# A streaming-encoder layer with a mixture of experts: short convolution in PSUM, VectorE alone converting weights late in the mixers, the first experts' chunks converted earlier, GpSimd out of the routing

## The chip, the core and the metric

The kernel runs on one core of a Trainium2 chip. The metric is the device time of one execution in microseconds (us). The engines in the text are TensorE (PE; its weight loads are PEld), VectorE (DVE), ScalarE (ACT), GpSimd (POOL) and SyncE (SP), whose queue issues every weight transfer.

## What is computed

One layer over 256 frames of width 1024. Three mixers read the same input projection, are gated and summed, and go through one output projection; a layer norm follows, and then 16 experts, two of which each frame uses.

```python
a  = a_val * sigmoid(a_gate)                       # branch A, "A" chunks
a  = silu(layer_norm(conv31(a) + conv_a_b))        # 31 taps per channel
yb = gate_bb * conv3(gate_cc * xb)                 # branch B, "X" and "B" chunks
pooled = trailing means over 2/4/8/16 minus self   # branch C, "C" chunks
merged = g0 * (a @ w_a_out) + g1 * (yb @ w_b_out) + g2 * (pooled @ w_c) * c_scale
x = layer_norm(ALPHA * x + merged @ w_o + b_o)
probs = softmax(x @ w_router + b_router)           # best group, best 2 in it
y = sum over e of combine[:, e] * (silu(x @ w_gate[e]) * (x @ w_up[e])) @ w_down[e]
x = layer_norm(ALPHA * x + y)
```

## The kernel before, in words

All weights are cut into chunks of 128 x 2048 float32 (1 MB), in the order of use: 49 for the mixers (`MIX`), 96 for the experts (`EXP`, six for each). Mixer chunks 0 to 7 are "A", 8 to 11 "C", 12 to 23 four times X, X, B, 24 is "WC", 25 to 36 four times G1, G2, WB, 37 to 40 "G0", and 41 to 48 WA, WA, WO, WA, WA, WO, WO, WO.

A chunk is not multiplied as it comes. It is split into a rounded half (H, `hi`, a copy on ACT, line 162) and the rest (L, `lo`, a subtraction, line 172), and TensorE multiplies three pairs: H with both halves of the activations, L with one. One mixer chunk is 48 matmuls of 256 columns (lines 314 and 319). `convert` runs two chunks ahead of the products; with `CUT = 1280` GpSimd subtracts 1024 + 256 of the 2048 columns and VectorE 768. Exceptions are the "native" chunks: the second half of every expert's down projection but the last is multiplied unsplit, as float32, by `mm_native` (line 1022).

In the mixers VectorE also evaluates the 31-tap convolution, one instruction for one tap of 128 channels (lines 333 and 336, accumulating in PSUM in tiles "z"). The taps wait in a list, and `drain` hands out as many for each chunk as a budget of 5.0 us less the chunk's own cost (`COST`) allows. The short convolution of branch B is done in `ev_X`: a product into u (line 396), then three taps from u into a tile y in SBUF (lines 400 and 402); `ev_B` multiplies the gate in (line 407). At chunk `LNA` (32) the taps that remain are handed out, and the layer norm of branch A follows at set distances from there (`ln_a`: line 458 to 487); its result AH, AL is the operand of the WA chunks. Up to line 800 a scheduler reorders instructions within each engine's queue; from `manual_schedule` on, the order is as written.

Then comes the routing. Two tiles of 128 frames (t = 0, 1) get their output projection (`wo`), residual (`add1`), statistics, logits, softmax, choice of experts, and places; `gather2` collects the chosen frames, and the first expert starts. `warm_up` puts idle matmuls in between. `C0`, `C1`, `C2` are the first three converted expert chunks. In the expert loop ACT rounds and VectorE alone subtracts, each two instructions of 1024 columns for a chunk.

Weight slots: `give` puts a free slot's name into a list, and SP issues the next chunk's transfer into it, so a transfer starts when a slot comes free. Slots H0 to H2 and L0 to L2 hold the split halves until the routing; after that all slots are one pool.

Of the kernel before, what the change touches and what calls it, by code (L numbers as in the profile page):

```python
# [49 lines left out]
def native(j):  # L50

    return CHUNKS[j][0] == "ED" and CHUNKS[j][2] == 1 and CHUNKS[j][1] < NE - 1
# [60 lines left out]
def body(ctx, tc, w, xt, x, par, rows, out):  # L113
# [211 lines left out]
    CA = {}  # L325

    def conv_tap(i, k):

        src = UP[:, i, k:k + T]
        wk = P[:, PCW + i * TAPS + k:PCW + i * TAPS + k + 1]  # L330
        if k == 0:
            CA[i] = bank("z", (128, T))
            V.tensor_scalar(CA[i], src, wk, col(PCB, i), op0=OP.mult, op1=OP.add)
        else:
            ca = CA[i]
# [50 lines left out]
    yconv = {}  # L386
    Y = {}

    def ev_X(i, p):
        if i == 0:  # L390
            Y["h"], Y["l"] = slot("YH", [128, KT, T], F32R), slot("YL", [128, KT, T], F32R)
        cc = t2k([128, T])
        S.activation(cc, p[:, 0], AF.Identity, bias=col(PB, 24 + i))
        u = t2k([128, 2 + T])
        G.memset(u[:, :2], 0.0)
        V.scalar_tensor_tensor(u[:, 2:], p[:, 1], col(PB, 32 + i), cc, op0=OP.add, op1=OP.mult)  # L396
        if i % 2 == 0:
# [129 lines left out]
    LNA = 32  # L527
# [6 lines left out]
    COST = {"A": .45, "C": .7, "X": 1.3, "B": .9, "WB": .7, "WA": 1.3}  # L534
# [24 lines left out]
    def router_consts():  # L559
# [8 lines left out]
        pb = bank("pj", (128, 2, NE))  # L568
# [229 lines left out]
    acc = {}  # L798
    ctx.enter_context(tc.manual_schedule())
# [39 lines left out]
    dummy = small([128, 1])  # L839
    for h in range(2):  # L840
# [3 lines left out]
        stats1(0, 2 * h, 2 * h + 1)  # L844
    S.activation(dummy, X1[:, 0, :1], AF.Exp)
# [7 lines left out]
    convert(C0, 2048, 512)  # L853
    hold[0] = 3
# [6 lines left out]
    x1a(0, 1)  # L861
    logits(0, 0)
# [3 lines left out]
    softmax1(0, u0)  # L866
    x1b(0, 0)
# [3 lines left out]
    select(0)  # L871
    wo(NM - 2, 2, 1, 1)
# [35 lines left out]
    lo(C1, G, 0, 1024)  # L908
# [76 lines left out]
    def hidden(e):  # L985
# [13 lines left out]
        def parts():  # L999
            S.activation(HS[e][:, :, 0], HF[e], AF.Copy)  # L1000
# [104 lines left out]
    for e in range(NE + 1):  # L1105
# [44 lines left out]
        if e:  # L1150
            p0 = bank("pj", (128, 512))
            block(lambda j: mm(p0, lambda k: HS[e - 1][:, k], j, True, True), before=gu if e < NE else ())
            steps = [lambda: ev_down(e - 1, 0, p0)]
# [9 lines left out]
            p1 = block(lambda j: down1(e - 1, j, some), before=steps, between=parts)  # L1163
# [5 lines left out]
            last = [lambda e=e, p1=p1: ev_down1(e - 1, p1)]  # L1169
# [6 lines left out]
    p1 = block(lambda j: down1(NE - 1, j, None))  # L1176
    ev_down1(NE - 1, p1)
# [113 lines left out]
```

## Time and profile before

| | us |
|---|---|
| median of 3 runs (lowest, highest) | 633.08 (632.39, 633.84) |
| the profiled execution's own time | 633.34 |
| its span, first to last instruction | 631.6 |
| PE, PEld busy in it | 585.9, 485.5 |
| DVE, ACT, POOL busy in it | 569.9, 373.8, 254.1 |

Busy shares of the whole span say little here, since the stages have different limits. The table by stretches of time is to be read first: in each stretch the number of matmuls in brackets, against a stretch in which TensorE never waits, tells how much of it was lost; the granted clock tells how much of that was lost to a slower clock, and the waits tell whom TensorE waited for.

### The profile page before, as it was taken

The page shows a single profiled execution, that of the slowest core. Times are in us where ns is not written, and L with a number is a line of the kernel's source. Part 1 is how long each engine was busy: PE and PEld are TensorE (multiplying, and loading weights), DVE is VectorE, ACT ScalarE, POOL GpSimd, SP SyncE. Part 2 cuts the span into 40 slices and gives each one's busy share as a digit, 9 for nine tenths or more (in the row PEclk, how much of TensorE's full clock was granted, in tenths as well). Part 3 has the DMA queues.
Part 4 walks back from the last instruction along what each step waited for, and adds up shares of the span by engine and source line. Part 5 has one row for each costly group of instructions (what it writes and reads, how often), then busy time and mean ns, then how long its engine had stood idle before and what let it go on. Part 6 is the DMA issues. An engine that isn't in the chain of part 4 may idle for free. (4 is left out here: it accounts for less than half of the span.)

```text
span 631.6 us, 9552 instructions
## 1 busy us (share of the span) xinstructions
PE 585.9 (93%) x3556; PEld 485.5 (77%) x3556; DVE 569.9 (90%) x851; ACT 373.8 (59%) x536; POOL 254.1 (40%) x187
## 2 busy tenths in 40 slices
PE   8999999988799999799989897999999999999990
PEld 6999999978799999798776564766676666666650
DVE  5999999999996399997688989899999999999985
ACT  5644444344344455734336587688778887887861
POOL 3876998874499777966341004000000000000003
PEclk9999999989799999999979899999999999999996
DMA  8985354354357544596753588689979998999101
GB/s 314 421 348 195 141 174 160 134 183 150 134 201 267 191 171 174 188 377 218 315 200 130 204 313 326 246 323 382 423 302 371 381 420 319 388 379 352 67 1 71
DMA packets 24084, 158.77 MB, mean 251 GB/s; under 512 B 2784, under 2 KB 3040, under 8 KB 5472
## 3 DMA queue, kind: packets, MB, share of 16 engines
q1 hardware_dynamic: 24032, 158.10, 65.5%
q8 instruction: 30, 0.49, 0.3%
q14 instruction: 22, 0.18, 0.1%
HBM read 157.04 MB, written 1.05 MB: 250 GB/s over the span
## 5 line engine op out<-in xcount | busy, mean ns | idle before, releaser
L172 POOL TENSOR_TENSOR L<-R,H 128x1024 fp32r<-128x1024 f32 (+1 forms) x72 | 131.9, 1854 | 31.0 <-ACT H L162 30.7
L314 PE MATMUL pj<-XH,H 128*128 128x256 f32 x560 | 139.3, 286 | 3.2 <-DVE t2k L396 3.2
L314 PE MATMUL pj<-XL,H 128*128 128x256 f32 x560 | 139.0, 285 | 0.0
L162 ACT ACTIVATE H<-R 128x1024 fp32r<-128x1024 f32 (+1 forms) x84 | 78.6, 988 | 63.7 <-issue 34.0
L314 PEld LDWEIGHTS pj<-XH,H 128*128 128x128 f32 x560 | 108.8, 194 | 3.4 <-DVE t2k L396 3.4
L314 PEld LDWEIGHTS pj<-XL,H 128*128 128x128 f32 x560 | 108.8, 194 | 0.0
L336 DVE SCALAR_TENSOR_TENSOR z<-UP,par,z 128x256 f32<-128x256 f32 x232 | 97.3, 477 | 0.2
L1192 POOL TENSOR_TENSOR sm<-sm,mhalf 128x1 f32<-128x1 f32 x2 | 1.1, 552 | 227.0 <-DVE sm L1191 227.0
L319 PE MATMUL pj<-XH,L 128*128 128x256 f32 x560 | 78.6, 283 | 0.0
L319 PEld LDWEIGHTS pj<-XH,L 128*128 128x128 f32 x560 | 72.4, 192 | 0.0
L172 DVE TENSOR_TENSOR L<-R,H 128x768 fp32r<-128x768 f32 (+2 forms) x37 | 56.4, 1526 | 9.9 <-ACT H L162 9.9
L172 POOL TENSOR_TENSOR L<-S,H 128x1024 fp32r<-128x1024 f32 (+1 forms) x28 | 49.8, 1800 | 12.5 <-ACT H L162 12.5
L162 ACT ACTIVATE H<-S 128x1024 fp32r<-128x1024 f32 x28 | 28.0, 1049 | 22.2 <-POOL L L172 12.7
L979 ACT ACTIVATE t2k<-pj 64x512 f32<-64x512 f32 x32 | 19.1, 596 | 19.4 <-PE pj L972 17.2
L172 DVE TENSOR_TENSOR L<-S,H 128x768 fp32r<-128x768 f32 x14 | 22.6, 1616 | 3.9 <-ACT H L162 3.9
L267 POOL TENSOR_TENSOR AL<-UP,R 128x512 fp32r<-128x512 f32 x4 | 7.4, 1860 | 45.4 <-ACT R L266 45.4
L981 DVE TENSOR_TENSOR t2k<-pj,t2k 64x512 f32<-64x512 f32 x32 | 21.7, 677 | 1.8 <-ACT t2k L979 1.7
L1000 ACT ACTIVATE hs<-ssum 128x256 fp32r<-128x256 f32 x16 | 6.7, 417 | 22.5 <-DVE ssum L997 22.5
L1014 PEld LDWEIGHTS z<-t2k,pt 128*128 128x128 f32 x64 | 10.9, 188 | 11.4 <-ACT hs L1000 7.3
L1014 PE MATMUL z<-t2k,pt 128*128 128x512 f32 x64 | 18.9, 416 | 0.0
L314 PE MATMUL pj<-AH,H 128*128 128x256 f32 x64 | 17.1, 302 | 0.0
L314 PE MATMUL pj<-AL,H 128*128 128x256 f32 x64 | 17.0, 298 | 0.0
(479 smaller groups left out, 1458.1 us busy)
## 6 DMA issues: line engine op xcount, KB each, us to landing
R<-w SPq DMA_DIRECT2D x55, 1024.0 KB, 5.4
S<-w SPq DMA_DIRECT2D x24, 1024.0 KB, 5.5
H<-w SPq DMA_DIRECT2D x15, 1024.0 KB, 7.6
L<-w SPq DMA_DIRECT2D x7, 1024.0 KB, 6.6
XL<-w SPq DMA_DIRECT2D x6, 1024.0 KB, 7.7
XH<-w SPq DMA_DIRECT2D x6, 1024.0 KB, 8.1
AC<-w SPq DMA_DIRECT2D x6, 1024.0 KB, 7.0
AH<-w SPq DMA_DIRECT2D x6, 1024.0 KB, 7.9
```

What stands on the lines that cost most here:

```text
L162: S.activation(HI[j][:, o], raw[j][:, o], AF.Copy)
L172: eng.tensor_tensor(LO[j][:, o], raw[j][:, o], HI[j][:, o].bitcast(F32), op=OP.subtract)
L267: eng.tensor_tensor(dl, src, dh.bitcast(F32), op=OP.subtract)
L314: PE.matmul(p[:, c], h[:, o:o + 128], m[:, k0 + k], start=(n == 0), stop=False)
L319: PE.matmul(p[:, c], l[:, o:o + 128], ah[:, k0 + k], start=False, stop=(n == 3 * nk))
L336: V.scalar_tensor_tensor(AC[:, i] if k == TAPS - 1 else ca, src, wk, ca, op0=OP.mult, op1=OP.add)
L979: S.activation(t, p[64:], AF.Copy)
L981: V.tensor_tensor(GU[e, n], p[:64], t, op=OP.add)
L1000: S.activation(HS[e][:, :, 0], HF[e], AF.Copy)
L1014: PE.matmul(acc[t, b], PTs[e][:, t], YV[e, b][n], start=False, stop=(e == NE - 1 and n == 1))
L1192: G.tensor_tensor(mv[:, 2:3], mv[:, 1:2], mhalf, op=OP.pow)
```

## The change

`ev_X` writes the short convolution's sums to PSUM (`ZY`, two banks), and the 31-tap sums share two banks (`ZC`); `ev_B` evicts the B chunk with two ACT instructions and multiplies both halves with one VectorE instruction. From block `LNA` on (now 34) VectorE subtracts whole chunks, and GpSimd none. The slots XH, XL, AH, AL go to the split halves first. In the routing C0, C1 and C2 are rounded and subtracted earlier and by VectorE, and the normalization of tile 1 is VectorE's. The first half of expert 0's down projection becomes native too.

```diff
 def native(j):
-    return CHUNKS[j][0] == "ED" and CHUNKS[j][2] == 1 and CHUNKS[j][1] < NE - 1
+    k, e, half = (*CHUNKS[j], 0)[:3]
+    return k == "ED" and (e == 0 or half == 1 and e < NE - 1)
...
-    CA = {}
+    ZC = [bank("z", (128, 2, T)) for _ in range(2)]
+    ZY = [bank("z", (128, 2, T)) for _ in range(2)]
...
-            CA[i] = bank("z", (128, T))
-            V.tensor_scalar(CA[i], src, wk, col(PCB, i), op0=OP.mult, op1=OP.add)
+            V.tensor_scalar(ZC[i // 2 % 2][:, i % 2], src, wk, col(PCB, i), op0=OP.mult, op1=OP.add)
...
-        if i % 2 == 0:
-            yconv[i // 2] = t2k([128, 2, T])
-        y = yconv[i // 2][:, i % 2]
+        y = ZY[i // 2 % 2][:, i % 2]
...
     def ev_B(q, p):
-        y = yconv.pop(q)
+        y = t2k([128, 2, T])
         for n in range(2):
-            V.scalar_tensor_tensor(y[:, n], p[:, n], col(PB, 16 + 2 * q + n), y[:, n], op0=OP.add, op1=OP.mult)
+            S.activation(y[:, n], p[:, n], AF.Identity, bias=col(PB, 16 + 2 * q + n))
+        V.tensor_tensor(y, y, ZY[q % 2], op=OP.mult)
...
-    LNA = 32
+    LNA = 34
...
-    COST = {"A": .45, "C": .7, "X": 1.3, "B": .9, "WB": .7, "WA": 1.3}
+    COST = {"A": .45, "C": .7, "X": 2.2, "B": 0.9, "WB": .7, "WA": 1.3}
...
-            convert(j + 2, CUT)
+            convert(j + 2, CUT if j < LNA else 0)
...
             at(j + 2, router_consts, True)
+            at(j + 5, router_consts2, True)
...
         if c == ("G0", 3):
-            give("XH", "XL")
+            hfree.append("XH")
+            lfree.append("XL")
         if c == ("WA", 3):
-            give("AH", "AL")
+            hfree.append("AH")
+            lfree.append("AL")
...
+    hi(C0, 0, 2048, 1024)
+    lo(C0, V, 0, 1024)
     for h in range(2):
...
         stats1(0, 2 * h, 2 * h + 1)
+        if h == 0:
+            lo(C0, V, 1024, 2048)
+            hi(C1, 0, 2048, 1024)
...
-    convert(C0, 2048, 512)
...
     x1a(0, 1)
+    lo(C1, V, 0, 1024)
     logits(0, 0)
...
     softmax1(0, u0)
+    hi(C2, 0, 2048, 1024)
...
     select(0)
+    add1(1, 0)
+    stats1(1, 0, 1)
+    lo(C1, V, 1024, 2048)
...
+    x1a(1, 1)
+    x1b(1, 0)
     u1 = shift1(1)
     softmax1(1, u1)
-    V.tensor_scalar(r1[1][:, 1:], r1[1][:, :1], -1.0, None, op0=OP.mult)
-    x11 = x1g(1, 1)
-    next(x11)
-    x1b(1, 0, 0, 256)
+    x1b(1, 1)
     S.activation(dummy, ex[1][:, :1], AF.Sigmoid)
-    hi(C1, 0, 1024)
-    next(x11)
-    next(x11)
-    lo(C1, G, 0, 1024)
...
     places(0, 1, 0, 2)
-    x1b(1, 0, 256, 512)
+    lo(C2, V, 0, 512)
     give("PH")
-    hi(C1, 1024, 2048, eng=V)
...
         def parts():
+            if e == 0:
+                return
...
-    lo(C1, V, 1024, 2048)
-    hold[0] = 4
+    hold[0] = HOLD2
     give()
-    hi(C2, 0, 2048)
-    lo(C2, G, 0, 1024)
-    lo(C2, V, 1024, 2048)
+    lo(C2, V, 512, 1024)
+    lo(C2, V, 1024, 2048, 1024)
```

`router_consts` is cut in two: its matmul and the two VectorE instructions behind it are `router_consts2`, three chunks later. `HOLD2` is 4. The code of the down projection (`down`, `ev_down1`, `scatter`) takes either half as native now; for expert 0 its first half's scatter is two matmuls instead of four.

Line numbers shift by a few in the changed kernel: line 172 becomes 173, 336 becomes 337, 400 and 402 become 398 and 400, 407 becomes 406, 473 becomes 472, 481 becomes 480, 486 and 487 become 485 and 486.

VectorE's order at an X and a B chunk, before (L336 is a tap of the long convolution, L400 and L402 those of the short one, L407 the gate's product, L172 a conversion):

```order
L400 TENSOR_SCALAR t2k_1096<-t2k_1171,par 128x256
L336 SCALAR_TENSOR_TENSOR z_1385<-UP_132,par,z_1385 128x256
L336 SCALAR_TENSOR_TENSOR z_1383<-UP_132,par,z_1383 128x256
L336 SCALAR_TENSOR_TENSOR z_848<-UP_132,par,z_848 128x256
L407 SCALAR_TENSOR_TENSOR t2k_1096<-pj_1177,par,t2k_1096 128x256
L172 TENSOR_TENSOR L_114_1237<-R_68_722,H_113_1235 128x768
```

The same place now (z_173 is one of the banks `ZY`):

```order
L400 SCALAR_TENSOR_TENSOR z_173<-t2k_1166,par,z_173 128x256
L173 TENSOR_TENSOR L_113_1232<-R_70_724,H_112_1230 128x768
L337 SCALAR_TENSOR_TENSOR z_172<-UP_132,par,z_172 128x256
L337 SCALAR_TENSOR_TENSOR z_171<-UP_132,par,z_171 128x256
L406 TENSOR_TENSOR t2k_1239<-t2k_1239,z_173 128x512
```

The short convolution's taps now write PSUM; the gate's product is one instruction of 512 columns, behind a conversion and two taps.

VectorE's order in branch A's layer norm, before (L473 reads the variance that TensorE has just summed, L481 scales all of A, L486 and L487 belong to the swish):

```order
L473 TENSOR_SCALAR t2k_2755<-pj_2740 128x256
L172 TENSOR_TENSOR L_242_2744<-R_203_2288,H_241_2742 128x768
L475 RECIPROCAL t2k_2756<-t2k_2754 128x256
L477 TENSOR_TENSOR t2k_2754<-t2k_2756 128x256
L478 SCALAR_TENSOR_TENSOR t2k_2754<-t2k_2755,t2k_2754 128x256
L479 SCALAR_TENSOR_TENSOR t2k_2756<-t2k_2754,t2k_2756 128x256
L481 TENSOR_TENSOR AC_170<-AC_170,t2k_2756 128x2048
L172 TENSOR_TENSOR L_260_2845<-R_208_2360,H_259_2843 128x768
L486 TENSOR_SCALAR t2k_2816<-AC_170,par 128x256
```

And now, from the same instruction to the first of the swish:

```order
L472 TENSOR_SCALAR t2k_2873<-pj_2859 128x256
L173 TENSOR_TENSOR L_248_2863<-S_209_2414,H_247_2861 128x1024
L474 RECIPROCAL t2k_2874<-t2k_2872 128x256
L476 TENSOR_TENSOR t2k_2872<-t2k_2874 128x256
L477 SCALAR_TENSOR_TENSOR t2k_2872<-t2k_2873,t2k_2872 128x256
L478 SCALAR_TENSOR_TENSOR t2k_2874<-t2k_2872,t2k_2874 128x256
L480 TENSOR_TENSOR AC_170<-AC_170,t2k_2874 128x2048
L173 TENSOR_TENSOR L_266_2963<-S_214_2487,H_265_2961 128x1024 x2
L485 TENSOR_SCALAR t2k_2934<-AC_170,par 128x256
```

Between the variance and the last swish there stood four conversions of 768 columns, and there stand nine of 1024 now; TensorE's sum of the squares has moved from five chunks ahead of the first WA chunk to three.

VectorE's order behind the places of tile 1, before:

```order
L758 TENSOR_TENSOR sm_3760<-pj_3757,sm_3755 128x16
L813 TENSOR_TENSOR ps<-sm_3760,slotn 128x256
L680 SCALAR_TENSOR_TENSOR UP_2994<-UP_2994,sm_3671,PH_2998 128x256
L160 CAST H_380_3712<-XH_3136 128x512 x2
L267 TENSOR_TENSOR YH_3687<-pj_3688,YH_3687 128x4x64 x2
L267 TENSOR_TENSOR YH_3687<-pj_3693,YH_3687 128x4x64 x2
L813 TENSOR_TENSOR ps<-sm_3660,slotn 128x256
L813 TENSOR_TENSOR ps<-sm_3760,slotn 128x256
L172 TENSOR_TENSOR L_381_3717<-XH_3136,H_380_3712 128x512 x2
L172 TENSOR_TENSOR PH_3799<-XL_3138,H_393_3794 128x512 x2
```

And now (L267 and L268 take the gathered frames out of PSUM, which the first expert's matmuls wait for; L680 normalizes):

```order
L764 TENSOR_TENSOR sm_3742<-pj_3739,sm_3737 128x16
L820 TENSOR_TENSOR ps<-sm_3742,slotn 128x256
L173 TENSOR_TENSOR L_387_3753<-R_290_3180,AL_3562 128x512
L268 TENSOR_TENSOR YH_3679<-pj_3680,YH_3679 128x4x64 x2
L268 TENSOR_TENSOR YH_3679<-pj_3685,YH_3679 128x4x64 x2
L820 TENSOR_TENSOR ps<-sm_3652,slotn 128x256
L820 TENSOR_TENSOR ps<-sm_3742,slotn 128x256
L173 TENSOR_TENSOR L_387_3753<-R_290_3180,AL_3562 128x512
L173 TENSOR_TENSOR L_387_3753<-R_290_3180,AL_3562 128x1024
```

The normalization and the two copies ahead of the gathered frames are gone from here, one conversion of 512 columns stands in their place, and behind them one of 512 and one of 1024 columns stand where there were four of 512.

## Rows read from the trace of the kernel before

**Rows 1.** The page's first line.

```profile
span 631.6 us, 9552 instructions
```

**Rows 2.** Windows: length; PE, PEld, DVE, ACT, POOL busy (count); clock, DMA share, GB/s.

```profile
20.00:130.00 110.00, 110.00 (x918) 109.89 (x916) 110.00 (x206) 49.92 (x65) 92.58 (x67) 1.00 0.58 218
130.00:170.00 40.00, 30.76 (x218) 30.26 (x218) 40.00 (x75) 15.30 (x23) 22.20 (x16) 0.87 0.46 161
195.00:222.00 27.00, 27.00 (x226) 26.95 (x225) 11.91 (x7) 12.49 (x17) 22.11 (x14) 1.00 0.59 214
222.00:260.00 38.00, 37.01 (x307) 36.78 (x306) 36.22 (x29) 23.25 (x36) 29.90 (x19) 1.00 0.46 167
260.00:270.00 10.00, 5.60 (x35) 5.42 (x34) 9.57 (x8) 6.56 (x12) 9.81 (x8) 0.83 0.74 260
318.00:335.00 17.00, 13.81 (x97) 12.53 (x98) 13.85 (x41) 6.31 (x14) 6.53 (x6) 0.80 0.45 183
335.00:395.00 60.00, 53.64 (x226) 35.71 (x226) 55.73 (x83) 43.34 (x63) 10.06 (x6) 0.95 0.68 258
395.00:600.00 205.00, 202.28 (x874) 137.69 (x873) 196.77 (x247) 163.50 (x231) 0.00 (x0) 1.00 0.85 335
```

**Rows 3.** TensorE's waits, whole span: who, for whom, total us, times, longest.

```profile
PE pj L422 <- DVE t2k L396: 6.1, 2, 5.1
PE pj L936 <- DVE ps L813: 5.0, 6, 2.8
PE pj L569 <- DVE t2k L567: 4.4, 1, 4.4
PE pj L314 <- DVE t2k L396: 3.2, 1, 3.2
PE pj L957 <- DVE R L267: 2.2, 1, 2.2
```

**Rows 4.** VectorE's groups, 20 to 305 us: count, busy us, mean ns, idle before.

```profile
L336 DVE SCALAR_TENSOR_TENSOR z<-UP,par,z 128x256 f32<-128x256 f32 x229 | 95.9, 477 | 0.1
L172 DVE TENSOR_TENSOR L<-R,H 128x768 fp32r<-128x768 f32 x33 | 51.3, 1554 | 9.1 <-ACT H L162 9.1
L402 DVE SCALAR_TENSOR_TENSOR t2k<-t2k,par,t2k 128x256 f32<-128x256 f32 x16 | 15.8, 985 | 0.0
L400 DVE TENSOR_SCALAR t2k<-t2k,par 128x256 f32<-128x256 f32 x8 | 8.8, 1104 | 0.0
```

**Rows 5.** VectorE's groups, 20 to 305 us: the layer norm of branch A.

```profile
L486 DVE TENSOR_SCALAR t2k<-AC,par 128x256 f32<-128x256 f32 x8 | 7.2, 924 | 0.3
L481 DVE TENSOR_TENSOR AC<-AC,t2k 128x2048 f32<-128x2048 f32 x1 | 4.4, 4374 | 0.0
```

**Rows 6.** Groups of the whole span: one conversion of 1024 columns with GpSimd at rest.

```profile
L172 DVE TENSOR_TENSOR PH<-XL,YL 128x1024 fp32r<-128x1024 f32 x4 | 4.8, 1222 | 0.0
```

**Rows 7.** Timeline of VectorE in the routing: start, us, what.

```profile
317.93 0.17 DVE L715 TENSOR_TENSOR sm<-sm,thr 128x16 f32<-128x16 f32 x1
...
326.42 1.27 DVE L715 TENSOR_TENSOR sm<-sm,thr 128x16 f32<-128x16 f32 x1
...
327.79 1.25 DVE L742 SCALAR_TENSOR_TENSOR sm<-sm,sm,sm 128x16 bf16<-128x16 f32 x1
...
329.51 1.00 DVE L813 TENSOR_TENSOR ps<-sm,slotn 128x256 fp32r<-128x256 f32 x1
```

**Rows 8.** Chain that ended last: start, us; native chunk, scatter, two split chunks.

```profile
573.06 3.58 PE pj L1022 x8
576.64 1.13 PE z L1014 x4
577.76 3.74 PE pj L972 x16
```

**Rows 9.** Other engines' waits, whole span: in total us, times, longest us.

```profile
ACT H L162 <- issue: 37.8, 12, 6.3
...
SPq L147 <- DVE L L172: 235.7, 49, 8.3
```

More of the change, by code (lines that the diff above doesn't have):

```diff
@@ L331, in conv_tap @@
         if k == 0:
-            CA[i] = bank("z", (128, T))
-            V.tensor_scalar(CA[i], src, wk, col(PCB, i), op0=OP.mult, op1=OP.add)
+            V.tensor_scalar(ZC[i // 2 % 2][:, i % 2], src, wk, col(PCB, i), op0=OP.mult, op1=OP.add)
         else:
-            ca = CA[i]
+            ca = ZC[i // 2 % 2][:, i % 2]
             V.scalar_tensor_tensor(AC[:, i] if k == TAPS - 1 else ca, src, wk, ca, op0=OP.mult, op1=OP.add)
@@ L384, in ev_C @@
         put("G", 10, mean)
-    yconv = {}
     Y = {}
@@ L567, in router_consts, with router_consts2 @@
         V.tensor_reduce(bs[:, 1], gw.rearrange("p k e -> p e k"), axis=AX.X, op=OP.add)
-        pb = bank("pj", (128, 2, NE))
+        RT["bs"] = bs
+    def router_consts2():
+        pb, bs = bank("pj", (128, 2, NE)), RT["bs"]
         PE.matmul(pb, ones, bs, start=True, stop=True)
@@ L798, in body @@
     acc = {}
+    HOLD, HOLD2 = 3, 4
     ctx.enter_context(tc.manual_schedule())
@@ L852, in body @@
     wo(NM - 3, 1, 1, 1)
-    convert(C0, 2048, 512)
-    hold[0] = 3
+    hold[0] = HOLD
     free.extend(hfree)
@@ L878, in body @@
             acc[t, b] = bank("z", (128, 512))
-    add1(1, 0)
     turn(1, 0)
-    stats1(1, 0, 1)
     warm_up(8)
@@ L1011, in scatter @@
         for t in range(2):
-            if not b or e == NE - 1:
+            if b and e < NE - 1 or e == 0:
+                PE.matmul(acc[t, b], PTs[e][:, t], YV[e, b], start=False, stop=False)
+            else:
                 for n in range(2):
                     PE.matmul(acc[t, b], PTs[e][:, t], YV[e, b][n], start=False, stop=(e == NE - 1 and n == 1))
-            else:
-                PE.matmul(acc[t, 1], PTs[e][:, t], YV[e, 1], start=False, stop=(e == NE - 1))
     def mm_native(e, j, p, mid):
@@ L1023, in mm_native, with down @@
         used(j)
-    def down1(e, j, mid):
-        if e == NE - 1:
+    def down(e, b, j, mid=None):
+        if not native(j):
             p = bank("pj", (128, 512))
@@ L1031, in down1, with ev_down1 @@
             p = bank("pj", (64, 512))
-            mm_native(e, j, p, mid)
+            mm_native(e, j, p, mid or (lambda: None))
         return p
-    def ev_down1(e, p):
-        if e == NE - 1:
-            ev_down(e, 1, p)
+    def ev_down1(e, b, p):
+        if p.shape[0] == 128:
+            ev_down(e, b, p)
             return
-        y = YV[e, 1] = t2k([128, 512], F32R)
+        y = YV[e, b] = t2k([128, 512], F32R)
         S.activation(y[:64], p, AF.Copy, scale=CW[e][:64])
@@ L1150, in body @@
         if e:
-            p0 = bank("pj", (128, 512))
-            block(lambda j: mm(p0, lambda k: HS[e - 1][:, k], j, True, True), before=gu if e < NE else ())
-            steps = [lambda: ev_down(e - 1, 0, p0)]
+            p0 = block(lambda j: down(e - 1, 0, j), before=gu if e < NE else ())
+            steps = [lambda: ev_down1(e - 1, 0, p0)]
             parts = ()
@@ L1162, in body @@
                 break
-            p1 = block(lambda j: down1(e - 1, j, some), before=steps, between=parts)
+            p1 = block(lambda j: down(e - 1, 1, j, some), before=steps, between=parts)
             if e < 2:
@@ L1168, in body @@
             scatter(e - 1, 0)
-            last = [lambda e=e, p1=p1: ev_down1(e - 1, p1)]
+            last = [lambda e=e, p1=p1: ev_down1(e - 1, 1, p1)]
         else:
@@ L1175, in body @@
     S.activation(y, p0, AF.Copy, scale=CW[NE - 1])
-    p1 = block(lambda j: down1(NE - 1, j, None))
-    ev_down1(NE - 1, p1)
+    p1 = block(lambda j: down(NE - 1, 1, j))
+    ev_down1(NE - 1, 1, p1)
     for t in range(2):
```

## The prediction, made before the changed kernel had run

> **What bounds the kernel now.** I read the windows by stage first. In a stretch in which TensorE never waits it gives 918 matmuls in 110 us, 8.35 per us, so a mixer chunk of 48 takes 5.75 us; VectorE is busy for the whole of that stretch too [rows 2]. Against this pitch two stretches of the mixers fall short. From 130 to 170 us there are 218 matmuls where 334 would fit, 116 missing or 13.9 us, at a granted clock of 0.87; from 222 to 270 us there are 342 in 48 us, 59 missing or 7.0 us, most of it behind 260 at 0.83 [rows 2]. The list of TensorE's waits says for whom: L314 and L422 wait 3.2 and 6.1 us for the product L396 of an X chunk (8 of those 9 us in two waits), and L569, the little matmul of `router_consts`, waits 4.4 us for L567 [rows 3]. In each VectorE is late, not TensorE. From 195 to 222 us VectorE is busy for 11.9 of 27 us [rows 2]: its work is unevenly spread.
>
> Why VectorE is late is in its groups. A tap of 128x256 that accumulates in PSUM costs 95.9/229 = 0.42 us (instructions overlap, so the time of the group counts, not the mean). The same shape from SBUF to SBUF costs 0.99 (L402) and 1.10 us (L400), and a conversion of 768 columns 1.55, while one of 1024 columns takes 1.22 with GpSimd at rest [rows 4, 6]. What VectorE does in SBUF alone is thus stretched to about twice beside GpSimd, and what has an operand in PSUM is not.
>
> In the routing, at a clock of 0.80 from 318 to 335 us, the same shows: L715 takes 0.17 us for tile 0 and 1.27 for tile 1, where GpSimd normalizes [rows 2, 7]. From 335 to 395 us VectorE is busy for 55.7 of 60 us, and TensorE waits for it 2.2 us at L957 and up to 2.8 at L936 [rows 2, 3]. From 395 us on TensorE and VectorE stand close to their limits (202.3 and 196.8 of 205 us) and the clock is 1.00 [rows 2]; the change leaves this stage alone.
>
> **The X and B chunks.** I count VectorE's work for the twelve conversions of chunks 16 to 27. Before: 95 taps and 15 products with a PSUM operand at 0.42, 46.2 us; 16 of L402, 15.8; 8 of L400, 8.8; 12 conversions at 1.55, 18.6; together 89.4 us [rows 4]. TensorE needs 12 x 5.75 = 69.0, so VectorE is 20.4 over, of which 13.9 came out as loss and 6.5 was taken up by the lead that it had. Now: 93 taps, 8 of L396 and the 24 short taps, all with a PSUM operand, 125 x 0.42 = 52.5; 4 of L406, which have twice the columns, 3.4; the conversions 18.6; together 74.5 us, 5.5 over, less than the 6.5 that the lead took up. So the waits should all but go. The 24 short taps are a shape that the trace does not hold in PSUM: 0.42 is the nearest row (same columns, PSUM written), 0.99 the other end. I take 0.42 and leave up to 2 us of loss: **gain 12**, between 8 and 13.9.
>
> What is moved for it: ACT gets 8 evictions. At 15.3/23 = 0.67 us for an ACT instruction there [rows 2] this is 5.3 us on an engine with 24.7 idle us in the 40, hidden unless they come late (a rival, below). The taps that are given out later land in VectorE's idle 15 us of 195 to 222. GpSimd keeps its conversions to chunk 33. SP's queue issues the same chunks in the same order.
>
> **Branch A's layer norm.** The matmul of `router_consts` waits three chunks less deep, so L569's 4.4 us leave, with the clock that they cost. But the layer norm starts two chunks later and more stands in it. VectorE's order is now: the variance (0.42), nine conversions of 1024 columns at 1.22 = 11.0, four small ones at up to 0.92 (L486's time, nearest in shape) = 3.7, the scaling of all A, which took 4.4 beside GpSimd and should take 2 x 1.22 = 2.4 without it, eight of L485 at 0.92 = 7.4 [rows 4 to 6], and the last piece's split, another 0.9: 25.8 us until the last of AL. Without GpSimd L485 shrinks, by its columns down to 0.3; so I take 25. TensorE has in the meantime three gate chunks, 17.25 us, and the matmuls of the first WA chunk that need only finished eighths of AH and AL, about 42, 5.0 us; together 22.3. It waits some 2.7 us where it lost 7.0. **Gain 4**, between 1.5 (an extra op or two in the chain and a slow clock behind the wait) and 7.
>
> The conversions from chunk 36 on cost VectorE 2 x 1.22 against 1.55, 0.9 us more for each; with no taps left it has 5.75 us for each chunk, so this is hidden outside the layer norm.
>
> **The routing.** L715 and L742 of tile 1 lose about 1.1 and 1.0 us (to L715's value of tile 0 and the same ratio), L813 some 0.6 [rows 7], all on the chain from the logits to the places. The half normalization and the two copies of 512 columns ahead of L267 go and one conversion of 512 columns comes, about 0.7 us off; tile 1's first statistics stand in front of the last `wo` products instead of behind them, about 1.2 us. Against this the earlier conversions of C0 to C2 add pieces of 1.2 us between the steps of tile 0, most of them while VectorE waits for TensorE or ACT: 0 to 2 us lost. **Gain 4.5**, between 2.5 and 6; a clock of 0.80 gives some back if the gaps shrink.
>
> **The first experts.** VectorE loses from here half of C1, all of C2 (together about 3 x 1.22 = 3.7 us), and the conversion of expert 0's first down chunk, 2.4, with the split of its operand, 0.4; it gains 1.8 of the rest of C2. That is 4.7 us off its 55.7. TensorE pays for the native chunk 3.58 - 1.87 = 1.7 us (the chain shows one native chunk, and two split ones in 3.74) and saves 1.13 x 0.6 = 0.7 of the scatter [rows 8]: 1.0 more. The waits L957 and most of L936, 5.0 us, have VectorE behind them, and behind each the granted clock is lower: 0.95 over these 60 us is 3 us [rows 2, 3]. Of 8 us I take 4.5 as gained, less the 1.0: **gain 3.5**, between 1 and 6.5. Late next is the transfer: the DMA share is 0.68 there.
>
> **The sum.** 12 + 4 + 4.5 + 3.5 = 24.0. The profiled execution took 633.34 us (its span of 631.6 [rows 1] and 1.8 around it), so 609.3; the median of the runs is 0.26 lower, so **609.0 us**. All good ends give 600, all bad ends 620.
>
> **The rivals.** *The overhang moves instead of going.* The X stage keeps a wait as VectorE's list of late taps meets the layer norm, or the layer norm's chain is longer: gains of 6, 0, 4 and 3 make 620. For it: VectorE is busy without a gap up to 195 us, so anything late is handed on. Against it: 15 idle us from 195 to 222 [rows 2].
>
> *The short taps stay as long as they were*, since what is slow is the reading of u in SBUF beside GpSimd, not the writing. Then the X stage gains nothing but hiding: 633.0 - 12 = 621. Against it: a tap of the long convolution also reads SBUF, and takes 0.42 [rows 4].
>
> [...]
>
> *Slower: the gate of branch B waits for ACT.* L406 needs both of ACT's evictions, and they stand in ACT's queue behind copies of weights, ahead of which ACT stands up to 6.3 us (12 times, 37.8 us) for something that the profile doesn't name, by its place the transfer [rows 9]. VectorE's order is fixed: behind a waiting L406 stand taps and the next conversion, which TensorE needs. At the longest wait four such places cost 4 x (6.3 - 0.9) = 21.6 us, and each a slow clock of 5.2/2 = 2.6 us behind it (0.87 over 40 us is 5.2, for two waits [rows 2, 3]), 10.4: 32 lost in place of 13.9, +18, less the 12 of the other stages: **639**. It decides from a wait of 3.9 us at each of the four. Against it: a conversion and two taps stand between, 1.55 + 0.84 us, and that conversion needs an ACT copy itself.
>
> *The transfers become the bound.* Fewer chunks come in before the experts, as the halves' slots are kept from the pool. SP waits 235.7 us for slots, not for the rate [rows 9], and from 395 us on the queue moves 335 GB/s at a share of 0.85 [rows 2]. If that is the limit, the experts start earlier and end as before, but for the early waits: 630.
>
> **How the numbers follow.** My forecast, 602 to 617, has 0.68; the overhang that moves 0.15; the short taps as before 0.08; the transfers 0.04; the wait for ACT 0.03; and 0.02 for some other wait in the routing or the layer norm that eats everything. 0.2% is 1.3 us, about what a measurement here can tell from no change. Of the transfers a half falls within it or above, as do the last two: faster 0.93, same 0.02, slower 0.05. A range of 600 to 621 holds the forecast, the overhang's case and about half of the short taps', and leaves out the rest.
>
> **What would show it.** Right: no wait for L396 and a clock of 1.00 from 130 to 170 us; L398 and L400 near 0.42; no L569 in the list of waits; one wait of at most 3 us ahead of the first WA chunk; L715's and L742's successors near 0.2 us for tile 1; the first expert's matmul some 20 us earlier (318 to 335 becomes about 300 to 312); native matmuls in expert 0. Wrong: L406 waiting for ACT, taps that stand in the layer norm, TensorE waiting in the experts for transfers.

## The result, and the profile after

Four runs each on one chip: the changed kernel 612.58 us (610.62 to 614.90), the kernel before 633.46 (632.39 to 635.25); ratio 0.9669, interval 0.9623 to 0.9715, or 20.9 us faster. The forecast was 609.0 in 600 to 621. Of its four terms two held, one was 2 us too small, and one, of 4 us, came out as nothing.

The profiled execution took 614.90 us, the slowest of the four. Its stretches, with the columns of [rows 2]:

```profile
130.00:170.00 40.00, 40.00 (x335) 40.00 (x335) 40.00 (x87) 21.62 (x34) 29.93 (x21) 1.00 0.57 202
...
222.00:250.00 28.00, 25.84 (x201) 25.46 (x201) 24.41 (x25) 17.76 (x25) 4.36 (x3) 0.94 0.53 187
250.00:270.00 20.00, 17.67 (x124) 16.39 (x124) 16.22 (x23) 11.43 (x19) 6.83 (x7) 0.91 0.65 233
...
375.00:580.00 205.00, 201.96 (x869) 137.46 (x868) 195.62 (x245) 162.24 (x228) 0.00 (x0) 0.99 0.85 335
```

From 130 to 170 us TensorE is whole: 335 matmuls where there were 218, clock 1.00 where it was 0.87. From 222 to 270 us it is not: 325 matmuls, where before there were 342 [rows 2], in a stretch that has other matmuls in it too, but at a clock of 0.94 and 0.91 (0.50 from 232 to 234 us and from 256 to 258). The experts behind 375 us run as they did.

Who TensorE waits for, as in [rows 3]:

```profile
PE pj L944 <- DVE ps L820: 4.7, 5, 2.8
PE pj L306 <- ACT XH L267: 2.3, 1, 2.3
PE pj L467 <- DVE t2k L462: 2.2, 1, 2.2
...
PE pj L315 <- POOL AL L268: 1.4, 2, 1.2
...
PE pj L315 <- ACT AH L267: 0.8, 1, 0.8
```

The waits for L396 and L569 are gone. New at their place: 2.2 us for L462, the reduction ahead of the variance (1.0 in the kernel before), and 2.0 for one of the eighths in which A comes (1.2 for AL and 0.8 for AH). L944 is the old L936, and its 2.8 us are still there.

VectorE's groups from 20 to 305 us, as in [rows 4]:

```profile
L337 DVE SCALAR_TENSOR_TENSOR z<-UP,par,z 128x256 f32<-128x256 f32 x232 | 98.8, 480 | 0.7
...
L400 DVE SCALAR_TENSOR_TENSOR z<-t2k,par,z 128x256 f32<-128x256 f32 x16 | 7.6, 478 | 0.0
...
L398 DVE TENSOR_SCALAR z<-t2k,par 128x256 f32<-128x256 f32 x8 | 3.8, 475 | 0.0
```

The short taps cost 7.6 + 3.8 = 11.4 us, where they cost 15.8 + 8.8 = 24.6 [rows 4]: 0.475 us each, near the mean of a long tap.

To see where the 18.5 us between the two spans came from, I take the same matmul in both timelines of TensorE (start in us, duration). After:

```profile
16.30 0.28 PE L315 MATMUL pj<-XL,H 128*128 128x256 f32 x1
...
165.94 0.28 PE L315 MATMUL pj<-YH,H 128*128 128x256 f32 x1
...
296.30 0.27 PE L663 MATMUL pj<-ident,UP 128*128 128x128 f32 x1
...
317.30 0.50 PE L980 MATMUL pj<-H,YH 128*128 128x512 f32 x1
...
362.74 0.64 PE L1032 MATMUL pj<-L,ssum 128*64 128x512 f32 x1
...
387.85 0.64 PE L1032 MATMUL pj<-AC,ssum 128*64 128x512 f32 x1
```

And before:

```profile
14.86 0.28 PE L314 MATMUL pj<-XL,H 128*128 128x256 f32 x1
...
178.62 0.28 PE L314 MATMUL pj<-YH,H 128*128 128x256 f32 x1
...
308.17 0.27 PE L657 MATMUL pj<-ident,UP 128*128 128x128 f32 x1
...
333.62 0.50 PE L972 MATMUL pj<-H,YH 128*128 128x512 f32 x1
...
382.50 0.64 PE L1022 MATMUL pj<-L,ssum 128*64 128x512 f32 x1
...
406.53 0.64 PE L1022 MATMUL pj<-AC,ssum 128*64 128x512 f32 x1
```

The differences of the starts, and what each stretch gained by itself:

| from the stretch's first matmul to its last | ahead at its end, us | gained in it | forecast |
|---|---|---|---|
| start to the first matmul of chunk 1 | -1.4 | -1.4 | 0 |
| to the first WB chunk (A, C, X, B) | 12.7 | 14.1 | 12 |
| to the first transposition of tile 0 (layer norm of A, WA, WO) | 11.9 | -0.8 | 4 |
| to the first expert (routing) | 16.3 | 4.4 | 4.5 |
| to the native chunk of expert 1 | 19.8 | 3.4 | 3.5 |
| to the native chunk of expert 2 | 18.7 | -1.1 | 0 |
| to the end of the span | 18.5 | -0.2 | 0 |

The 1.4 us at the start are no part of the change: TensorE's first wait there, for ACT's XH, is 2.3 us here, and one of 2.1 stands in the profile of a kernel below that has this stretch as before.

### The profile page after: what moved, and what is told of

It reads as the page before. It is cut to its first block, busy times and chain, and to the rows that moved or that the text cites. A ratio compares the mean times of both kernels' runs of the same rounds, so it can differ in the third digit from the quotient of the medians.

```text
span 613.1 us, 9493 instructions
## 1 busy us (share of the span) xinstructions
PE 581.2 (95%) x3554; PEld 481.7 (79%) x3554; DVE 545.1 (89%) x862; ACT 373.8 (61%) x536; POOL 194.3 (32%) x150
## 5 line engine op out<-in xcount | busy, mean ns | idle before, releaser
L163 ACT ACTIVATE H<-R 128x1024 fp32r<-128x1024 f32 (+1 forms) x74 | 72.2, 1027 | 67.2 <-issue 30.0
L173 POOL TENSOR_TENSOR L<-R,H 128x1024 fp32r<-128x1024 f32 (+2 forms) x50 | 88.0, 1783 | 21.2 <-ACT H L163 21.2
L173 DVE TENSOR_TENSOR L<-R,H 128x768 fp32r<-128x768 f32 (+2 forms) x46 | 62.7, 1378 | 11.5 <-ACT H L163 11.5
L163 ACT ACTIVATE H<-S 128x1024 fp32r<-128x1024 f32 x30 | 30.1, 1050 | 29.2 <-issue 16.6
L173 POOL TENSOR_TENSOR L<-S,H 128x1024 fp32r<-128x1024 f32 (+1 forms) x20 | 36.6, 1855 | 1.1 <-ACT H L163 1.1
L173 DVE TENSOR_TENSOR L<-S,H 128x768 fp32r<-128x768 f32 (+1 forms) x16 | 24.1, 1519 | 5.5 <-ACT H L163 5.4
L268 POOL TENSOR_TENSOR R<-UP,YL 128x512 fp32r<-128x512 f32 x4 | 7.4, 1858 | 54.4 <-ACT YL L267 54.4
L944 PEld LDWEIGHTS pj<-ps,YL 128*128 128x128 f32 x48 | 8.8, 206 | 10.8 <-DVE ps L820 3.9
L268 POOL TENSOR_TENSOR AL<-t2k,AH 128x256 fp32r<-128x256 f32 x8 | 9.0, 1136 | 25.7 <-ACT AH L267 25.7
L944 PE MATMUL pj<-ps,YL 128*128 128x256 f32 x48 | 11.9, 321 | 5.2 <-DVE ps L820 4.7
```

What stands on the lines that cost most here:

```text
L163: S.activation(HI[j][:, o], raw[j][:, o], AF.Copy)
L173: eng.tensor_tensor(LO[j][:, o], raw[j][:, o], HI[j][:, o].bitcast(F32), op=OP.subtract)
L268: eng.tensor_tensor(dl, src, dh.bitcast(F32), op=OP.subtract)
L944: PE.matmul(p[:, n], xs[:, t, (4 * b + k) * 128:(4 * b + k + 1) * 128], PS[:, t, :, 0], start=(t == 0), stop=(t == 1))
```

## The experiments

Twelve kernels, in three groups on one chip each, with the kernel before in each group. Ratios are to it. The first four take the change apart; the next four look into the layer norm, its pace and the last wait; the last four close what these left open.

**The short convolution alone.**

```diff
...
-        if i % 2 == 0:
-            yconv[i // 2] = t2k([128, 2, T])
-        y = yconv[i // 2][:, i % 2]
+        y = ZY[i // 2 % 2][:, i % 2]
...
-            V.scalar_tensor_tensor(y[:, n], p[:, n], col(PB, 16 + 2 * q + n), y[:, n], op0=OP.add, op1=OP.mult)
+            S.activation(y[:, n], p[:, n], AF.Identity, bias=col(PB, 16 + 2 * q + n))
+        V.tensor_tensor(y, y, ZY[q % 2], op=OP.mult)
...
-    COST = {"A": .45, "C": .7, "X": 1.3, "B": .9, "WB": .7, "WA": 1.3}
+    COST = {"A": .45, "C": .7, "X": 2.2, "B": 0.9, "WB": .7, "WA": 1.3}
```

> The kernel before with the X and B chunks' part of the change alone. Theory (the gains are each stage's own and add up): the waits for L396 go, the stretch from 130 to 170 us shows about 334 matmuls at a clock of 1.00, the first YH matmul comes 12 to 14 us earlier, and all of it stays to the end: 620 us, ratio 0.979. Rival (the taps that are handed out later only move the overhang to the layer norm of branch A, and it takes the later LNA to keep the gain): 626 us or more, with TensorE's wait ahead of the first AH matmul grown by what is missing.

Measured: 617.83 us, ratio 0.9762 (0.9731 to 0.9792), 15.2 us faster, where the theory's 620 were 13. The window from 130 to 170 us:

```profile
130.00:170.00 40.00, 40.00 (x336) 40.00 (x335) 40.00 (x86) 21.33 (x35) 29.32 (x21) 1.00 0.55 192
```

TensorE is whole again, and the layer norm ahead of the first AH matmul waits no longer than before (L569's successor 4.4 us). The rival falls: with LNA 32 no wait at the layer norm grew by the late taps.

**The mixers' late part alone.**

```diff
-    LNA = 32
+    LNA = 34
...
-            convert(j + 2, CUT)
+            convert(j + 2, CUT if j < LNA else 0)
...
+            at(j + 5, router_consts2, True)
```

> The kernel before with the mixers' late part alone: LNA 34, no GpSimd conversions behind it, router_consts cut in two. Theory, formed from the changed kernel's trace (this part is worth nothing, since the wait for L462, 2.2 us, two waits for the last eighths of A, 2.0 us, and a second stretch at half clock take the place of the 4.4 us at L569): 633 us, ratio 0.997 to 1.003. Rival (it is worth the 4 us of the prediction, and the loss seen in the changed kernel came from the short convolution's later taps): 629 us, ratio 0.994, with the wait for the variance at 1 us as before.

Measured: 632.15 us against 633.06, ratio 0.9999 (0.9977 to 1.0021). The theory holds, the prediction's 4 us don't. TensorE's waits:

```profile
PE pj L468 <- DVE t2k L463: 2.1, 1, 2.1
PE pj L305 <- ACT XH L266: 2.1, 1, 2.1
```

L569 is gone from the list and L468 <- L463 (the variance) stands at 2.1 us with no short convolution in PSUM, so the longer wait is this part's own.

**The routing and the first experts alone** (the diff from `native` and from the slots of the halves on, with the mixers as before):

```diff
...
+    k, e, half = (*CHUNKS[j], 0)[:3]
+    return k == "ED" and (e == 0 or half == 1 and e < NE - 1)
...
-            give("XH", "XL")
+            hfree.append("XH")
+            lfree.append("XL")
...
+    hi(C0, 0, 2048, 1024)
+    lo(C0, V, 0, 1024)
...
```

> The kernel before with the routing's and the first experts' part alone (early C0 to C2, no GpSimd there, native first half of expert 0, slots of the halves kept). Theory by the changed kernel's trace (4.4 us from the logits to the first expert, 3 in the first expert, 1 given back behind it): 626.7 us, ratio 0.990. Rival (the prediction's sum of 4.5 and 3.5): 625.0, ratio 0.987; other rival (the gain of the experts depends on the earlier start of the transfers that the mixers' gain gives): 629.

Measured: 624.81 us, ratio 0.9880 (0.9841 to 0.9919), 8.2 us faster by the medians and 7.6 by the ratio. That is the prediction's sum of 4.5 and 3.5; the theory from the timelines (6.4) is inside the interval too, the third (4) just outside.

**The changed kernel without the short convolution's part** (the first diff, backwards):

```diff
...
-        y = ZY[i // 2 % 2][:, i % 2]
+        if i % 2 == 0:
+            yconv[i // 2] = t2k([128, 2, T])
+        y = yconv[i // 2][:, i % 2]
...
```

> The changed kernel with the X and B chunks' part undone. If the parts add up: 612.6 + 13 = 625.5 us, ratio to before 0.988. If the later layer norm also relieves VectorE in the X stage (two chunks more in which to hand out taps): 620 us or less. The waits for L396 are back, 9 us in all, in the first case.

Measured: 625.21 us, ratio 0.9882 (0.9845 to 0.9918): as the routing alone. Against the changed kernel's 0.9669 the short convolution is worth 0.0213 or 13.5 us. The waits for L396 (L397 in this kernel) are back within a tenth, 6.1 and 3.1 us:

```profile
PE pj L423 <- DVE t2k L397: 6.1, 2, 5.1
```

So the later layer norm didn't relieve VectorE in the X stage. The product of the three parts' ratios, 0.9762 x 0.9999 x 0.9880 = 0.9644, lies in the whole's interval: the parts add up as far as these runs can tell.

**GpSimd keeps subtracting** (in the changed kernel):

```diff
-            convert(j + 2, CUT if j < LNA else 0)
+            convert(j + 2, CUT)
```

> The changed kernel, but GpSimd keeps subtracting its 1280 columns up to the end of the mixers. Theory (GpSimd's rest is what the late layer norm needs, since its SBUF operations are stretched beside it): the scaling of A takes 4.4 instead of 2.3 us and the swish 0.9 instead of 0.5 for each of 16, less what the shorter conversions give back, so the waits ahead of the first AH products grow from 2 to 5 us or more: 617 us, ratio to before 0.974. Rival (the conversions that VectorE took over cost as much as they free): 612.6, ratio 0.967, and TensorE's waits in the layer norm no longer than in the changed kernel.

Measured: 616.94 us, ratio 0.9721 (0.9689 to 0.9752), as the theory has it. VectorE's groups around the layer norm with GpSimd at work:

```profile
L486 DVE TENSOR_TENSOR t2k<-t2k,t2k 128x256 f32<-128x256 f32 x8 | 7.3, 927 | 0.9 <-ACT t2k L484 0.7
L485 DVE TENSOR_SCALAR t2k<-AC,par 128x256 f32<-128x256 f32 x8 | 5.4, 697 | 0.1
...
L480 DVE TENSOR_TENSOR AC<-AC,t2k 128x2048 f32<-128x2048 f32 x1 | 4.4, 4381 | 0.0
```

And in the changed kernel, where it rests but for the halves of A:

```profile
L486 DVE TENSOR_TENSOR t2k<-t2k,t2k 128x256 f32<-128x256 f32 x8 | 4.2, 549 | 0.0
L485 DVE TENSOR_SCALAR t2k<-AC,par 128x256 f32<-128x256 f32 x8 | 4.1, 540 | 0.7 <-POOL AL L268 0.6
...
L480 DVE TENSOR_TENSOR AC<-AC,t2k 128x2048 f32<-128x2048 f32 x1 | 2.3, 2293 | 0.0
```

The same three groups take 17.1 us and 10.6. TensorE's waits for the eighths are 3.9 and 2.2 us here, where they were 1.4 and 0.8. So GpSimd's rest is worth 3 to 4 us (0.9721 against 0.9669). The two intervals overlap by 0.0026; it is the groups and the waits that tell the kernels apart. The wait for L462, 2.2 us in the changed kernel, is 0.7 here. That the whole late part is worth nothing means that something else in it costs as much.

**LNA 33** (in the changed kernel):

```diff
-    LNA = 34
+    LNA = 33
```

> The changed kernel with LNA 33: the layer norm starts a chunk (5.75 us) earlier. Theory (the two waits for the last eighths, 2.0 us, and the slow clock behind them, 1.7, are there only because the chain starts too late; the wait for L462 stays): 609 us, ratio 0.961. Rival (the taps that must be out a chunk earlier come back as waits for L396 or as a longer wait for L462): 612 to 615.

Measured: 606.92 us, ratio 0.9562 (0.9532 to 0.9592), clear of the changed kernel's interval by 0.003 and 1.1% below it in the middle. TensorE's waits:

```profile
PE pj L467 <- DVE t2k L462: 0.7, 1, 0.7
PE pj L315 <- POOL AL L268: 0.7, 1, 0.7
```

And the stretch of the layer norm, of which the changed kernel has two windows at clocks of 0.94 and 0.91 (above):

```profile
222.00:270.00 48.00, 46.65 (x365) 45.10 (x365) 44.33 (x53) 29.61 (x45) 11.29 (x10) 1.00 0.67 241
```

More went than the theory had: the wait for L462 shrank to 0.7 too, and the clock is 1.00. So it is the place of the layer norm that cost what GpSimd's rest gave. (`LNA` also sets the chunk from which GpSimd rests, so this run moves that by a chunk too.) No wait for L396 came back.

**The squares first** (in the changed kernel):

```diff
-        at(j + 1, squares)
+        at(j + 1, squares, None)
...
+        for f in extra.pop((j, None), ()):
+            f()
         if j + 2 < NM:
             convert(j + 2, CUT if j < LNA else 0)
```

> The changed kernel with the reduction of the squares (L462) put ahead of its block's conversion, which takes 3.5 us beside GpSimd. Theory (it is this conversion that makes TensorE wait 2.2 us for the variance, and the whole chain late): the wait goes with the 1.7 us of slow clock behind it, and the waits for the last eighths shrink: 607 to 609 us, ratio 0.96. Rival (the conversion is then late for its own chunk, or ACT's copies set the pace of the eighths): 611 to 613, with TensorE waiting for an L173.

Measured: 611.88 us, ratio 0.9642 (0.9600 to 0.9684): not to be told from the changed kernel. The edit did less than meant. L462 has to wait for ACT's squares, so the scheduler kept the conversion ahead of it, and only L443 moved behind the reduction:

```profile
223.56 2.36 DVE L173 TENSOR_TENSOR L<-R,H 128x1024 fp32r<-128x1024 f32 x2 [0.94 <-ACT H L163]
225.84 3.82 DVE L462 TENSOR_REDUCE t2k<-PH 128x256 f32<-128x2048 f32 x1
```

The wait for L462 fell to 1.1 us, those for the eighths stayed (2.2). So the theory was not put to the test; of the rival, ACT's copies do set the pace of an eighth, as shown in the part on the prediction.

**The places first** (in the changed kernel; `todo` is the list from which the blocks take small work):

```diff
             if e == 2:
+                todo += [lambda t=t: places(1, t) for t in range(2)]
                 todo.extend(lambda t=t, h=h: parts1(t, h) for t in range(2) for h in range(2))
...
-                todo += [lambda e=e, t=t: places(e // 4 + 1, t) for t in range(2)]
+                if e > 2:
+                    todo += [lambda e=e, t=t: places(e // 4 + 1, t) for t in range(2)]
```

> The changed kernel with the places of experts 4 to 7 (L820, two of 1.2 us) a few steps earlier in VectorE's order, ahead of the splitting of x and not right before the gathering that reads them. Theory (the wait of 2.8 us for L820, which the change left as it was, comes from this order, and the clock falls to its lower level for 6.8 us behind it): wait and slow clock go, 608 us, ratio 0.960. Rival (VectorE is the bound there, so that the wait turns up at another line): 612 us.

Measured: 613.38 us, ratio 0.9660 (0.9622 to 0.9698), no gain. The rival, but with another engine than it named:

```profile
PE pj L944 <- POOL H L268: 2.5, 2, 2.1
```

The longest wait for L820 is 0.9 us now. GpSimd's split of x was hardly earlier than VectorE's places, and is late next.

**The changed kernel without its late part** (the second diff, backwards):

```diff
-    LNA = 34
+    LNA = 32
...
-            convert(j + 2, CUT if j < LNA else 0)
+            convert(j + 2, CUT)
...
-            at(j + 5, router_consts2, True)
```

> The changed kernel with the mixers' late part undone: LNA 32, GpSimd subtracting to the end of the mixers, router_consts whole. If the late part is worth nothing beside the short convolution too: 612.6 us, ratio to before 0.967. If it costs what the two other parts together lack (15.2 and 8.2 us each by itself, 23.4, against 20.9 of the whole): 609.7 us, ratio 0.963, with L569's wait of 4.4 us back and no wait for the last eighths.

Measured: 611.71 us against 631.81, ratio 0.9674 (0.9645 to 0.9702), the changed kernel's 0.9669 again. Beside the short convolution the late part is worth nothing either. L568, the old L569, waits its 4.4 us for L566.

**The first half of expert 0's down projection converted again** (in the changed kernel):

```diff
-    k, e, half = (*CHUNKS[j], 0)[:3]
-    return k == "ED" and (e == 0 or half == 1 and e < NE - 1)
+    return CHUNKS[j][0] == "ED" and CHUNKS[j][2] == 1 and CHUNKS[j][1] < NE - 1
...
-            if e == 0:
-                return
...
-            if b and e < NE - 1 or e == 0:
+            if b and e < NE - 1:
```

> The changed kernel with the first half of expert 0's down projection converted again. By the prediction TensorE saves 1.0 us and VectorE gets 2.8 more in a stretch in which it was busy for 55.7 of 60 us before. Theory (VectorE has room there now, 34 of 40 us, but TensorE's waits hang on its order): 612 to 614 us, within 0.3% of the changed kernel. Rival (native is what removed the wait at the first expert): 616 or more, with the wait at the line of L965 back at 2.2 us or longer.

Measured: 610.00 us, ratio 0.9641 (0.9613 to 0.9668). Against 0.9669 this is 1.8 us faster or nothing; the intervals overlap. The wait at the first expert (L964 <- L267) stays 1.5 us, so the rival falls: it was not the native chunk that shortened it. From the first expert's matmul to expert 1's native chunk this profile has 44.4 us (315.2 to 359.6), the changed kernel's 45.4: the 1.0 us that the prediction charged TensorE for the native chunk, and VectorE's relief gave nothing for it.

**LNA 33 and the squares first** (in the changed kernel):

```diff
-        at(j + 1, squares)
+        at(j + 1, squares, None)
...
-    LNA = 34
+    LNA = 33
...
```

> The changed kernel with LNA 33 and the reduction of the squares ahead of its block's conversion. LNA 33 left 0.7 us of wait for L462 and 0.7 for the eighths. Theory (they go): 605.5 to 606.9 us. Rival (the conversion behind the reduction is late): 608.

Measured: 606.20 us, ratio 0.9581 (0.9554 to 0.9608). Not told from LNA 33 alone (0.9562); the waits of 0.7 us stayed. Inconclusive: in LNA 33 alone the reduction stands ahead of L443 already, so there was little to move.

**LNA 33, places first, and the split of x an expert earlier** (in the changed kernel):

```diff
-    LNA = 34
+    LNA = 33
...
+            if e == 1:
+                todo.extend(lambda t=t, h=h: parts1(t, h) for t in range(2) for h in range(2))
             if e == 2:
-                todo.extend(lambda t=t, h=h: parts1(t, h) for t in range(2) for h in range(2))
+                todo += [lambda t=t: places(1, t) for t in range(2)]
...
```

> The changed kernel with LNA 33, the places of experts 4 to 7 ahead of their gathering, and the split of x on GpSimd an expert earlier. In the run with the places alone the 2.8 us of wait went over to GpSimd's split. Theory (both must be early): no wait for L820 or for GpSimd's L268 there, the slow clock behind it gone: 603 to 604.5 us. Rival (the split takes two slots from the pool for an expert longer and the transfers come late): 607 or more, with TensorE waiting for chunks in experts 2 and 3.

Measured: 605.77 us, ratio 0.9587 (0.9559 to 0.9614), also as LNA 33 alone. The 2.8 us wait is gone, in its place are four of 0.6 at most for the places and one of 1.0 for ACT; and the clock is 1.00 to the last stage:

```profile
130.00:590.00 460.00, 446.72 (x2543) 350.12 (x2542) 415.15 (x617) 306.10 (x444) 81.67 (x56) 1.00 0.72 274
```

Yet nothing is gained that can be measured. Between the native chunks of experts 0 and 1, where the split of x now stands, its profile has 22.8 us, and LNA 33 alone 20.0; from there to expert 2's it has 20.2 against 24.0. What the second stretch gains, the first mostly takes; TensorE's small waits for ACT's and VectorE's halves of weights (0.2 to 0.4 us each) have come up in it. And its wait for an eighth of A is 1.8 us, where LNA 33 alone has 0.7. So of the versions run, LNA 33 alone is as good as any and beats both kernels.

## Why the prediction was right, and where it was not

**What bounds the mixers: right, a little small.** The reading of [rows 2 to 4] (VectorE late in the X stage since its SBUF operations are stretched beside GpSimd) gave 12 and up to 2 us of residue; the stretch gained 14.1, all of the loss, and the part alone 15.2 (interval 13.2 to 17.0). The value that was taken for the short taps in PSUM, 0.42, came out 0.475 (11.4/24), 1.3 us more in all, and the 5.5 us of overhang did not show as a wait.

That GpSimd is what stretches the operations in SBUF, the kernel before shows by itself. L402 took 0.47 us while GpSimd stood idle (the 8.36 us ahead of 153.25), and 2.17 beside one of its conversions:

```profile
149.88 0.47 DVE L402 SCALAR_TENSOR_TENSOR t2k<-t2k,par,t2k 128x256 f32<-128x256 f32 x1
...
158.88 2.17 DVE L402 SCALAR_TENSOR_TENSOR t2k<-t2k,par,t2k 128x256 f32<-128x256 f32 x1
```

```profile
153.25 0.10 POOL L395 MEMSET t2k<- 128x2 f32 x1 [8.36 <-DVE t2k L396]
...
157.71 3.92 POOL L172 TENSOR_TENSOR L<-S,H 128x1024 fp32r<-128x1024 f32 x2
```

Left open is how the gain divides. Three edits lie in this part (the sums in PSUM, the gate's evictions on ACT, the higher cost of an X chunk in `COST`), and no run takes them apart. By the first matmul of the first WB chunk 38 taps of the long convolution were still to start, where there had been 25 before: 13 taps, or 5.5 us at 0.42, that VectorE did later without making TensorE wait, beside the 13.2 by which the short taps shrank.

In the changed kernel too an operation of 256 columns from SBUF to SBUF is short with GpSimd at rest (it stood idle for the 20.73 us ahead of 247.87), 0.43 us:

```profile
238.22 0.43 DVE L478 SCALAR_TENSOR_TENSOR t2k<-t2k,t2k 128x256 f32<-128x256 f32 x1
```

The 0.99 and 1.10 of [rows 4] are means over instructions with and without GpSimd at work beside them; from 130 to 170 us it worked for 22.2 of 40 [rows 2].

**The layer norm of A: the term that failed.** The step was: TensorE "waits some 2.7 us where it lost 7.0. Gain 4". The 7.0 held all that the stretch lost: L569's 4.4 us, 1.0 ahead of the variance, and the slow clock (10 us at 0.83, 1.7). The 2.7 held one wait alone. Left out of it was the clock, which stands in the low end of the range alone: the windows from 222 to 270 us show 28 x 0.06 + 20 x 0.09 = 3.5 us lost by it. And left out was the wait ahead of the variance, not among the rows; it is 2.2 us now, for L462 behind a conversion that VectorE does whole and that takes 3.46 us for two halves, as GpSimd is at work at L444 (2.23 us from 224.90; two halves at 240.89, with GpSimd idle, take 2.35, and in the run with the squares first, where L443 stands behind them, 2.36; with GpSimd kept, where L462 stands ahead of that conversion, the wait is 0.7):

```profile
224.75 3.46 DVE L173 TENSOR_TENSOR L<-R,H 128x1024 fp32r<-128x1024 f32 x2
228.14 3.74 DVE L462 TENSOR_REDUCE t2k<-PH 128x256 f32<-128x2048 f32 x1
...
233.27 0.42 DVE L472 TENSOR_SCALAR t2k<-pj 128x256 f32<-128x256 f32 x1 [0.26 <-PE pj L467]
```

The wait that the sum did hold came out at 2.0 us, near its 2.7, by luck. The sum let TensorE wait for the last of AL; for that it waited 0.18 us, behind products of the next chunk. The 0.8 and 1.2 are for the fourth eighth and not, as the expectations have it, for the last ones. Its rounded half (the fourth L267 of eight) stood on ACT right behind two copies of weights, and GpSimd subtracts the rest after that:

```profile
251.34 1.99 ACT L163 ACTIVATE H<-R 128x1024 fp32r<-128x1024 f32 x2
253.23 0.40 ACT L267 ACTIVATE AH<-t2k 128x256 fp32r<-128x256 f32 x1
```

```profile
253.69 0.51 PE L315 MATMUL pj<-AH,H 128*128 128x256 f32 x2 [0.81 <-ACT AH L267]
255.41 0.51 PE L315 MATMUL pj<-AL,H 128*128 128x256 f32 x2 [1.22 <-POOL AL L268]
...
261.17 0.38 PE L315 MATMUL pj<-AL,H 128*128 128x256 f32 x1 [0.18 <-POOL AL L268]
```

The chain from L472 to the last of AL took 28.5 us (233.27 to 261.80), where the sum had 25.

2.2 + 2.0 + 3.5 = 7.7 us take the place of the 7.0, which is the -0.8 of the table. Two runs, with and without the other parts, put the term at zero (0.9999, with an interval from 1.5 us gained to 1.3 lost, and 0.9674 against 0.9669). Pairs of other runs show two things in it that go against each other. GpSimd's rest gives 3.3 us (0.9721 against 0.9669). A layer norm at 34 instead of 32, both times with GpSimd at work, costs 3.0 (0.9721 against 0.9674, with `router_consts` cut in the first). Each of the two is about as large as its noise. With the rest in place a start one chunk earlier gave 5.7 us by the medians (612.58 to 606.92) and 6.8 by the ratios; 3.0 of them are in the waits for L462 and for the eighths (each 2.2 in all at 34 and 0.7 at 33) and 3.5 in the clock. The cut of `router_consts` was not run by itself.

**The routing: right.** Forecast 4.5, gained 4.4. L721 and L820 of tile 1 take 0.17 and 0.42 us, where [rows 7] have 1.27 and 1.00, and L742's successor takes 0.23 for 1.25:

```profile
313.32 0.17 DVE L721 TENSOR_TENSOR sm<-sm,thr 128x16 f32<-128x16 f32 x1
...
314.73 0.42 DVE L820 TENSOR_TENSOR ps<-sm,slotn 128x256 fp32r<-128x256 f32 x1
```

These are 2.7 us. The rest of the term was not taken apart, and the routing was run together with the first experts alone, 8.2 us for the 8.0 of the two terms.

**The first experts: the size near, the reasons half.** 3.4 us came by the native chunk of expert 1, and 1.1 went back by that of expert 2; the forecast's stretch ended at 395 us, between the two. L957's wait fell from 2.2 to 1.5 us (L965 now), but of L936's 2.8, which the prediction counted whole among the 8 us of which it took 4.5, nothing went: it hangs on where the places stand in VectorE's order (put first, their longest wait is 0.9), and on GpSimd's split of x right behind (2.1 then). That the down chunk had to be native for the gain is not borne out; converted again it was no slower.

**The rivals.** None came. No wait for ACT at L406 is in the list; the short taps did not stay slow; the transfers did not bind (share 0.85 and 335 GB/s behind 375 us, as before). Of the overhang that moves to the layer norm, the part that came true is a wait there, and the run without the short convolution shows it was not the X stage's overhang.

## What to carry to other kernels

When two stretches are compared, charge the slow clock behind a wait to both or to neither; here waits of 2.2 and 2.0 us came to 7.7 with the clock behind them. In these runs a VectorE operation of 256 columns that read or wrote PSUM took 0.47 to 0.48 us beside a working GpSimd (L396, L398, L400; GpSimd busy for 29.93 of the 40 us from 130), and for the short taps that was worth over half of their time (24.6 us before, 11.4 now); GpSimd's rest gave 3.3 us in the layer norm, about as much as its noise, where VectorE's chain is what TensorE waits for. And before a chain is put later, follow it from its first link and on every engine that it passes: the gain of a faster chain was spent on its later start, and one number (LNA 33) gave it back, 5.7 us by the medians.

## What was not expected of the hardware

The same wait of 2.8 us ahead of the gathering for experts 4 to 7 was not followed by the same clock. TensorE's windows of 20 us around it, in the changed kernel, with LNA 33, and without the late part:

```profile
365.00:385.00 20.00, 17.11 (x72) 13.31 (x71) 18.16 (x22) 11.58 (x20) 5.46 (x4) 0.83 0.54 204
```

```profile
360.00:380.00 20.00, 16.92 (x83) 13.74 (x84) 18.30 (x23) 13.21 (x22) 4.05 (x3) 0.91 0.60 228
```

```profile
365.00:385.00 20.00, 16.69 (x88) 12.80 (x87) 19.42 (x25) 14.50 (x24) 3.71 (x2) 1.00 0.68 247
```

Clocks of 0.83, 0.91 and 1.00 are by estimate 6.8 (20 x 0.17 / 0.5), 3.6 and 0 us at a clock of 0.50, which the changed kernel shows from 375 to 378 us and which is taken for LNA 33 too, behind waits of the same length. So a part of the spread between runs, and of what a small edit seems to give, may be where the wait falls; that was not tried by itself. And the last run of the experiments, with no slow clock from 20 to 590 us, was not measurably faster than LNA 33 alone, which has such a stretch; it waited longer elsewhere.
